# Hybrid decoder block on one core: one product for both sines, gate biases once a block, row scaling by ScalarE, and the mLSTM's maxima spread over the partitions by TensorE

## The chip, the cores and the metric

One core of a Trainium2 chip runs the whole program. The metric is the device time of one execution in microseconds (us). Before the change the median of three runs is 2684.09 us (2683.67 to 2686.39). The engines are called as in the profile: PE (TensorE), DVE (VectorE), ACT (ScalarE), POOL (GpSimd) and SP (SyncE, which here only issues DMAs).

## What is computed

A decoder block over 2048 tokens of width 1024: normalised rows go through one wide projection, its parts through a sliding-window attention and an mLSTM side by side, and their gated sum and a SwiGLU follow. The change lies in the key, query and gate part of the projection. Cut to that, the reference is:

```python
h = modulate(rms_norm(x, g_pre_mix[l]), shift_m, scale_m)
proj = h @ w_in[l]
q_a, k_a, v_a, q_m, k_m, v_m, o_m, i_m, f_m, g_a, g_m = jnp.split(proj, split_points, axis=-1)
q_a = rope(q_a.reshape(B, S, N_Q_HEADS, HEAD_DIM), positions)
k_a = rope(k_a.reshape(B, S, N_KV_HEADS, HEAD_DIM), positions)
y_a = sliding_window_attention(q_a, k_a, v_a, attn_sinks[l])
i_pre = i_m + b_if[l][:MLSTM_HEADS]
f_pre = f_m + b_if[l][MLSTM_HEADS:]
h_m = mlstm_chunkwise(q_m, k_m, v_m, i_pre, f_pre)
...
def rope(t, positions):
    t1, t2 = tf[..., :half], tf[..., half:]
    return jnp.concatenate([t1 * cos - t2 * sin, t2 * cos + t1 * sin], axis=-1)
```

Inside the mLSTM a running maximum `m` of each of the 4 heads scales its exponentials; the kernel computes it as one row of 512 numbers a head and block, and needs the values at the ends of its 128-token chunks on all 128 partitions.

## The kernel before

The tokens are worked in 4 blocks of 512 (NT = 4 tiles of 128 each), and the first part of the kernel in two superblocks of two blocks: blocks 0 and 1 from about 58 to 700 us, blocks 2 and 3 from there. The second part, the SwiGLU, is not touched. All large products are made exact by splitting each operand into a high and a low half (`whi` by ACT at L266 or L263, `wlo` by DVE at L267 or L264) and three matmuls (`mm3`), so PE's instructions are mostly triples at L211 into four accumulators `acc`.

A superblock runs through `h` and the projections in this order: queries of the first block (`evac_q`), its keys, values and gates (`evac_kv`, 264 columns), the mLSTM's values (`vm`, evacuated by ACT at L819), then keys and queries of the second block. For each of these a token tile's accumulator is copied by ACT into a `tx` tile (9 buffers, L772, L798, L819), and for keys and queries `rope` (L738) turns it on DVE with five products: two with the sines of half the width (L749, L750), one with the cosines (L751), a difference and a sum (L752, L753). `evac_kv` also makes the difference of a tile's values to those of the tile before, which it keeps in the constant tile `v_last` (L802, L803), and adds the biases to the 4 + 4 gate columns, in two operations a tile (L804, L805). The halves of queries and keys and the values go to DRAM in `at_d` (L766, L793, L806, L808) and come back as one tile `at` a 128 tokens for the attention (L896).

`hprep` (L475) prepares the normalised rows of a block: sums of squares by ACT (L471), an inverse root by POOL (L457, `rs`), the scaling of four tiles of 128x1024 rows by DVE (L492), then PE's transposes and the affine step by ACT (L502 for the high half, L504) and DVE (L505, the low half). In the odd blocks it also makes sums and differences of parts of `h` (L518 to L521), which `hsums` copies into other tiles with a DMA (L529) and splits again with ACT (L535) and DVE (L536).

`gates` (L824) makes the log gates (L827 to L836), transposes them, runs the scan of the maxima on 4 partitions, and collects in `sm` (4x8) the maxima and sums at the chunks' ends. `sm` goes to DRAM (`sm_d`, L865) and is read back with every partition getting all 32 numbers (`mp`, L867). After a pause of `L_SCAN` PE transposes the rows (68 columns a tile), DVE copies them to `cl` (L875) and forms the exponents `ex` from `cl` and `mp` (L878 to L880), and ACT takes their exponential (L881).

`attention` computes the scores from `at` (copied from PSUM by ACT at L927, masked by DVE at L929), their maxima (L934 to L937), the exponentials on ACT (L942, and `es` at L938), their scaling on POOL (L946), and after PE's transposes of them (L216) the product with the values (L955, L968). Two streams of tiles run side by side.

The order is made in two steps. The Python program lays a main line of matmul triples and between them advances side streams (`gates`, `attention`, `hprep` and so on): each stream yields the time after which it is due again, on a clock `now` (L204) that every matmul and transpose advances by an assumed cost, and `tick` steps what is due. The instructions of ACT, DVE, PE and SP keep the program's order only up to L1557 (`pinned`); from there the build may reorder each engine's instructions by its own estimate of readiness, so an edit in one place can move others. Each engine then works strictly in its order. SP's queue holds nearly all DMAs, the prefetch of raw weights (L297) and of the gates' weights (L441) among them.

## Time and profile before

| | |
|---|---|
| median of 3 runs | 2684.09 us |
| the profiled execution, its time | 2684.71 us |
| its span in the profile | 2682.9 us |
| mean granted clock of PE | 0.993 |
| PE busy | 2628.5 us, 98% |
| DVE busy | 1970.2 us, 73% |
| ACT busy | 1298.3 us, 48% |
| POOL busy | 141.8 us, 5% |

The rows of the profile read: line, engine, operation, the tile written, the tiles read, their shape, the count, then the busy time in us, the mean length of one in ns, and the idle time of the engine just before them with what ended it. Rows of a stretch give the busy time of each engine in it, the granted clock of PE (1.00 is full speed), the busy share of the DMA engines and their GB/s. Neighbouring instructions of one engine overlap a little, so the start of one to the start of the next is shorter than the length shown.

### The profile page before, as it was taken

Reading aid. Unit: us, or ns where it says so; the run is one execution under the profiler, and the core shown is the slowest. Engines: PE = TensorE matmul, PEld = TensorE weight load, DVE = VectorE, ACT = ScalarE, POOL = GpSimd, SP = SyncE. Lnnn points to the kernel's source line nnn. Section 1 sums busy time; section 2 is a strip of 40 time slices with the busy share of each in tenths; the row PEclk is TensorE's granted clock in tenths of the full one; section 3 lists DMA queues with packets and bytes.
Section 4 is the critical chain, followed back from the end, with each engine's and each line's share of the span. In section 5 each row is a group of like instructions: output and inputs, shape, how many; then the busy total and the mean of one; then the engine's idle time right before and its main releaser. Section 6 shows DMA issues by size and latency. Waiting matters only on the chain.

```text
span 2682.9 us, 35853 instructions
## 1 busy us (share of the span) xinstructions
PE 2628.5 (98%) x12414; PEld 2139.1 (80%) x12414; DVE 1970.2 (73%) x3854; ACT 1298.3 (48%) x2527; POOL 141.8 (5%) x181
## 2 busy tenths in 40 slices
PE   8899999999998999999999999999999999999998
PEld 6677788888886778888878888888878888888876
DVE  5788887768686988876777777775776667676466
ACT  5566544545764754444654443335654333333444
POOL 1000001201101000110000000000000000000000
PEclk9899999999999999999999999999999999999999
DMA  7663456887575645578675555446675323234556
GB/s 257 193 229 131 152 180 188 282 315 240 189 253 163 208 133 166 184 246 328 218 249 175 180 170 180 137 150 216 217 244 185 107 101 108 97 110 138 195 199 219
DMA packets 353669, 511.89 MB, mean 191 GB/s; under 512 B 25152, under 2 KB 213692, under 8 KB 348240
## 3 DMA queue, kind: packets, MB, share of 16 engines
q1 hardware_dynamic: 335272, 493.82, 55.3%
q10 hardware_dynamic: 18216, 15.79, 1.9%
q8 instruction: 98, 1.61, 0.2%
q14 instruction: 83, 0.68, 0.1%
HBM read 357.12 MB, written 144.02 MB: 187 GB/s over the span
## 4 chain that ended last, share of the span: by engine, by line
PE 62%; DVE 3%; DMA 2%; ACT 1%; issue 0%; POOL 0%; SPq 0%; DVEq 0%; POOLq 0%; ACTq 0%
PE acc L211 41%; PE mix L211 19%; DVE hl L1589 1%; PE mix L216 1%; DMA raw<-ws_d 1%; ACT hl L1588 1%; DMA raw<-as_d 0%; DMA raw<-in_w_ffn_down_dram 0%; DMA w<-x 0%; DVE w L1899 0%; DVE big L1589 0%; DMA raw<-in_w_ffn_gate_dram 0%; DVE big L1912 0%; DVE w L1932 0%; ACT big L1634 0%
## 5 line engine op out<-in xcount | busy, mean ns | idle before, releaser
L211 PE MATMUL acc<-big,hl 128*128 128x512 f32 x3936 | 933.8, 392 | 2.3 <-ACT hl L1588 0.7
L211 PEld LDWEIGHTS acc<-big,hl 128*128 128x128 f32 x3936 | 732.9, 188 | 165.6 <-issue 10.0
L1588 ACT CAST hl<-raw 128x512 fp32r<-128x512 f32 x732 | 440.0, 621 | 506.1 <-PE acc L211 235.7
L1589 DVE TENSOR_TENSOR hl<-raw,hl 128x512 fp32r<-128x512 f32 x732 | 498.4, 696 | 190.0 <-ACT hl L1588 187.8
L211 PE MATMUL acc<-whi,big 128*128 128x512 f32 (+1 forms) x1216 | 355.8, 374 | 9.5 <-ACT big L502 3.6
L211 PE MATMUL mix<-big,hl 128*128 128x512 f32 x1056 | 263.1, 390 | 1.6 <-ACT hl L1588 0.9
L211 PEld LDWEIGHTS acc<-whi,big 128*128 128x128 f32 x1216 | 221.8, 190 | 51.0 <-ACT big L502 3.9
L211 PE MATMUL acc<-hl,hl 128*128 128x512 f32 x1008 | 237.2, 393 | 5.9 <-DVE hl L1589 3.2
L211 PEld LDWEIGHTS mix<-big,hl 128*128 128x128 f32 x1056 | 197.7, 188 | 44.5 <-DVE hl L1589 1.9
L211 PEld LDWEIGHTS acc<-hl,hl 128*128 128x128 f32 x1008 | 187.0, 188 | 51.7 <-DVE hl L1589 8.4
L211 PE MATMUL acc<-wlo,big 128*128 128x512 f32 (+1 forms) x608 | 226.0, 374 | 2.2 <-DVE wlo L267 2.2
L211 PE MATMUL mix<-hl,hl 128*128 128x512 f32 x792 | 182.9, 391 | 3.1 <-DVE hl L1589 1.3
L211 PEld LDWEIGHTS mix<-hl,hl 128*128 128x128 f32 x792 | 147.7, 188 | 37.7 <-DVE hl L1589 4.7
L211 PE MATMUL acc<-big,whi 128*128 128x512 f32 x512 | 157.9, 393 | 0.0
L267 DVE TENSOR_TENSOR wlo<-raw,whi 128x1024 fp32r<-128x1024 f32 (+1 forms) x95 | 108.3, 1141 | 65.0 <-ACT whi L266 59.0
L266 ACT CAST whi<-raw 128x1024 fp32r<-128x1024 f32 (+1 forms) x95 | 93.7, 986 | 109.9 <-PE acc L211 103.8
L211 PEld LDWEIGHTS acc<-wlo,big 128*128 128x128 f32 x608 | 115.4, 190 | 23.3 <-DVE wlo L267 3.8
L457 POOL TENSOR_TENSOR rs<-ms,halves 128x1 f32<-128x1 f32 (+1 forms) x56 | 44.0, 798 | 1639.5 <-DVE ms L455 1630.6
L211 PE MATMUL mix<-hcT4h,hl 128*128 128x512 f32 x352 | 115.6, 389 | 0.7 <-ACT hl L1588 0.7
L211 PE MATMUL acc<-hcT2h,hl 128*128 128x512 f32 x352 | 115.5, 389 | 0.0
L211 PEld LDWEIGHTS acc<-big,whi 128*128 128x128 f32 x512 | 95.4, 188 | 19.2
L211 PE MATMUL acc<-big,wlo 128*128 128x512 f32 x256 | 97.6, 392 | 0.0
(354 smaller groups left out, 3520.9 us busy)
## 6 DMA issues: line engine op xcount, KB each, us to landing
raw<-in_w_in_dram SPq DMA_DIRECT2D x46, 1024.0 KB
as_d<-w SPq DMA_DIRECT2D x154, 256.0 KB
raw<-as_d SPq DMA_DIRECT2D x70, 512.0 KB
raw<-in_w_ffn_gate_dram SPq DMA_DIRECT2D x22, 1024.0 KB
raw<-in_w_ffn_up_dram SPq DMA_DIRECT2D x22, 1024.0 KB
raw<-ws_d SPq DMA_DIRECT2D x40, 512.0 KB
tx<-in_w_ada_dram SPq DMA_DIRECT2D x64, 256.0 KB
g_d<-tx SPq DMA_DIRECT2D x64, 256.0 KB
```

The source lines that it names most:

```text
L211: T.matmul(o, lhsT=lhsT, rhs=rhs, start=start, stop=stop, skip_group_check=resumed)
L216: T.transpose(o, i, ident[:k, :k])
L266: A.copy(hv, src)
L267: V.tensor_tensor(lv, src, hv.bitcast(F32), op=ALU.subtract)
L457: G.tensor_tensor(r[:, :n], ms[:, :n], nhalf[:, :n], op=ALU.pow)
L1588: A.copy(v(hi), src)
L1589: V.tensor_tensor(v(lo), src, v(hi).bitcast(F32), op=ALU.subtract)
```

## The change

Five edits in one diff. (1) In `rope` the two products with the sines become one over the full width; its input is read with the two halves of each head swapped (a step of -1 in that dimension) and the sines are broadcast over both. (2) In `evac_kv` the gate columns are copied raw by ACT into `gt` (two small copies a tile), and `gates` adds both biases for all four tiles in two operations. (3) The difference of values takes the tile before from its own `tx` buffer; only the block's last tile is copied to `v_last`, by ACT. (4) In `hprep` the scaling of rows goes from DVE to ACT. (5) In `gates` the DRAM tile `sm_d` and its two DMAs go: DVE spreads `sm` along a diagonal (`own`, 4x32, zeros elsewhere), one matmul with a matrix of ones puts the sum over the 4 partitions, which is all 32 numbers, on every partition, and DVE copies it from PSUM to `mp`.

```diff
--- before.py
+++ after.py
@@ -489,7 +489,7 @@
                 xb = xbs[i]
                 r = rms_of_rows(xb, vs[i])
                 for t in range(2):
-                    V.tensor_scalar(xb[:, t, :], xb[:, t, :], r[:, t:t + 1], None, op0=ALU.mult)
+                    A.activation(xb[:, t, :], xb[:, t, :], AF.Copy, scale=r[:, t:t + 1])
                     xs.append(xb[:, t, :])
         yield L_HP1[1] if b == 1 else L_X
 
@@ -742,12 +742,11 @@
             raw = raw[:, :W]
             src = raw.rearrange("p (h u f) -> p h u f", u=2, f=32)
             cb = cos[:, t, :].unsqueeze(1).to_broadcast([P, heads * 2, 32])
-            sb_ = sin[:, t, :].unsqueeze(1).to_broadcast([P, heads, 32])
+            sb_ = sin[:, t, :].unsqueeze(1).unsqueeze(1).to_broadcast([P, heads, 2, 32])
             z = tx([P, 512])
             zz = z[:, :W].rearrange("p (h u f) -> p h u f", u=2, f=32)
             rr = raw.rearrange("p (h f) -> p h f", f=32)
-            V.tensor_tensor(zz[:, :, 0, :], src[:, :, 1, :], sb_, op=ALU.mult)
-            V.tensor_tensor(zz[:, :, 1, :], src[:, :, 0, :], sb_, op=ALU.mult)
+            V.tensor_tensor(zz, src[:, :, ::-1, :], sb_, op=ALU.mult)
             V.tensor_tensor(rr, rr, cb, op=ALU.mult)
             V.tensor_tensor(src[:, :, 0, :], src[:, :, 0, :], zz[:, :, 0, :], op=ALU.subtract)
             V.tensor_tensor(src[:, :, 1, :], src[:, :, 1, :], zz[:, :, 1, :], op=ALU.add)
@@ -793,16 +792,21 @@
                     nc.sync.dma_start(at_d[n_][:, AT_K:AT_V].rearrange("p (i u k) -> p i u k", i=2, u=2)[:, :, u, :], kk.bitcast(F32))
 
         def evac_kv(b):
+            before = [v_last]
+
             def evac(t, ps):
                 raw = tx([P, 392])
                 A.copy(raw[:, :264], ps[:, :264])
                 v, dv = raw[:, 128:256], raw[:, 264:392]
                 n = b * NT + t
                 y = rope(raw, HKV, b, t)
-                V.tensor_tensor(dv, v, v_last, op=ALU.subtract)
-                V.tensor_copy(v_last, v)
-                V.tensor_tensor(gt[:, t, 0:4], raw[:, 256:260], b_if[:, 0:4], op=ALU.add)
-                V.tensor_tensor(gt[:, t, 32:36], raw[:, 260:264], b_if[:, 4:8], op=ALU.add)
+                for i in range(2):
+                    A.copy(gt[:, t, 32 * i:32 * i + 4], raw[:, 256 + 4 * i:260 + 4 * i])
+                V.tensor_tensor(dv, v, before[0], op=ALU.subtract)
+                before[0] = v
+                if t == NT - 1:
+                    A.copy(v_last, v)
+                    before[0] = v_last
                 nc.sync.dma_start(at_d[n][:, AT_V + P:], dv)
                 if n + 1 < S // P:
                     nc.sync.dma_start(at_d[n + 1][:, AT_V:AT_V + P], v)
@@ -822,6 +826,9 @@
 
 
         def gates(b):
+            for i in range(2):
+                g_ = gt[:, :, 32 * i:32 * i + 4]
+                V.tensor_tensor(g_, g_, b_if[:, 4 * i:4 * i + 4].unsqueeze(1).to_broadcast([P, NT, 4]), op=ALU.add)
             fv = gt[:, :, 32:36]
             e_, u_, d_, l_, n_ = [small.tile([P, NT, 4], F32, tag=f"sp{i}", name=nm("sp"), bufs=1) for i in range(5)]
             V.scalar_tensor_tensor(e_, fv, -1.0, fv, op0=ALU.mult, op1=ALU.min)
@@ -860,15 +867,16 @@
             V.tensor_copy(m_last, mend[:, 3:4])
             V.tensor_copy(sm[:, 4:8], rw[32:36, :].rearrange("p (c t) -> p c t", t=P)[:, :, P - 1])
             negm_d = tc.dram_tile([MH, TB], F32, name=nm("negm_d"))
-            sm_d = tc.dram_tile([MH, 8], F32, name=nm("sm_d"))
             nc.sync.dma_start(negm_d, rw[32:36, :])
-            nc.sync.dma_start(sm_d, sm)
+            own = lf[:, :MH * 8].rearrange("p (h k) -> p h k", h=MH)
+            V.tensor_tensor(own, sm.unsqueeze(1).to_broadcast([MH, MH, 8]), ident[:MH, :MH].unsqueeze(2).to_broadcast([MH, MH, 8]), op=ALU.mult)
             mp = small.tile([P, MH, 8], F32, tag="mp", name=nm("mp"), bufs=2)
-            nc.sync.dma_start(mp, sm_d.unsqueeze(0).to_broadcast([P, MH, 8]))
             yield L_SCAN
             pc_ = mix_tile()
             for t in range(NT):
                 transpose(pc_[:, t * 68:(t + 1) * 68], rw[:, t * P:(t + 1) * P])
+            mm(pc_[:, NT * 68:NT * 68 + 32], ones[:MH, :], own.rearrange("p h k -> p (h k)"), True, True)
+            V.tensor_copy(mp.rearrange("p h k -> p (h k)"), pc_[:, NT * 68:NT * 68 + 32])
             cl = small.tile([P, NT, 3, 4], F32, tag="cl", name=nm("cl"), bufs=2)
             pv_ = pc_[:, :NT * 68].rearrange("p (t w) -> p t w", t=NT)
             for i in range(3):
```

The line numbers after the change are shifted: L492 stays, the sine product is L749, the cosines L750, `vm`'s evacuation L823 (was L819), the score copies L935 (L927), `ex` L886 to L889 (L878 to L881), `es` L946 (L938), the attention's exponentials L950 (L942), the `at` load L904 (L896) and the product's copy L963 (L955). The numbers behind the tiles' names count tiles and are not the same before and after.

How ACT's row reads in block 0, about 105 us into the run, around the exponential `ex` of the maxima and the eight exponentials of the attention's first tile (`tm_1058`, `tm_1059`; afterwards `tm_1047`, `tm_1048`); `mix_1215` (afterwards `mix_1206`) holds the transposed rows of `h` for block 1. Before:

```order
L266 CAST whi_1611<-raw_904 128x528
L881 ACT_TABLE_LOAD
L881 ACTIVATE ex_1133<-ex_1133 128x48
L927 COPY tm_1145<-mix_1165 128x256
L502 ACTIVATE big_966<-mix_1215,sh_162,s_159 128x512
L504 ACTIVATE big_745<-mix_1215,sh_162,s_159 128x512
L942 ACTIVATE tm_1058,sums_1056<-tm_1058,nmx_1055 128x128
L938 ACTIVATE es_1057<-es_1057 128x8
L942 ACTIVATE tm_1058,sums_1056<-tm_1058,nmx_1055 128x128 x3
L942 ACTIVATE tm_1059,sums_1056<-tm_1059,nmx_1055 128x128 x4
```

After:

```order
L266 CAST whi_1555<-raw_893 128x528
L823 COPY tx_1552<-acc_926 128x512
L950 ACT_TABLE_LOAD
L950 ACTIVATE tm_1047,sums_1045<-tm_1047,nmx_1044 128x128
L946 ACTIVATE es_1046<-es_1046 128x8
L950 ACTIVATE tm_1047,sums_1045<-tm_1047,nmx_1044 128x128 x3
L950 ACTIVATE tm_1048,sums_1045<-tm_1048,nmx_1044 128x128 x4
L935 COPY tm_1136<-mix_1156 128x256
L889 ACTIVATE ex_1124<-ex_1124 128x48
L502 ACTIVATE big_957<-mix_1206,sh_162,s_159 128x512
L504 ACTIVATE big_742<-mix_1206,sh_162,s_159 128x512
L266 CAST whi_1602<-raw_893 128x528
```

The attention's exponentials, with the load of their table, now stand ahead of `ex`, and `ex` ahead of L502 and L504, which stood ahead of the exponentials before.

SP's row in block 2, at about 761 us, from the load of the first `at` tile to the copies of `hsums` (L529, `big` to `big`). Before:

```order
L896 DMA at_7491<-at_d_198 128x1792
L297 DMA raw_7735<-in_w_in_dram 128x4x512
L793 DMA at_d_199<-tx_7392 128x2x128
L793 DMA at_d_200<-tx_7392 128x2x128
L806 DMA at_d_201<-tx_7433 128x128
L793 DMA at_d_200<-tx_7415 128x2x128
L793 DMA at_d_201<-tx_7415 128x2x128
L529 DMA big_8022<-big_6899 128x2048
L529 DMA big_8024<-big_6494 128x2048
```

After:

```order
L904 DMA at_7462<-at_d_198 128x1792
L529 DMA big_7995<-big_6881 128x2048
L297 DMA raw_7708<-in_w_in_dram 128x4x512
L792 DMA at_d_199<-tx_7368 128x2x128
L792 DMA at_d_200<-tx_7368 128x2x128
L792 DMA at_d_200<-tx_7389 128x2x128
L792 DMA at_d_201<-tx_7389 128x2x128
L529 DMA big_7997<-big_6476 128x2048
```

The first copy of `hsums` has moved from behind the raw weights (L297) and five stores to a place ahead of them; the second stays behind the stores of keys (L793, afterwards L792), and the store of a value difference (L806) has moved ahead of these rows.

ACT's row in block 3's `hprep`, at about 710 us, where L565 sums the squares of the previous superblock's output rows, L571 scales them and L263 splits the weights of the queries. Before:

```order
L565 ACTIVATE big_6619,sx_6950<-tx_6930 128x512
L565 ACTIVATE tm_6829,sx_6950<-tx_6932 128x512
L565 ACTIVATE big_6619,sx_6991<-tx_6965 128x512
L565 ACTIVATE tm_6848,sx_6991<-tx_6967 128x512
L565 ACTIVATE big_6619,sx_7029<-tx_7006 128x512
L565 ACTIVATE tm_6866,sx_7029<-tx_7008 128x512
L571 ACTIVATE big_6619<-tx_6844,rs_6928 128x512
L571 ACTIVATE tm_6814<-tx_6846,rs_6928 128x512
L263 CAST whi_6972<-raw_6773 128x2x4x64 x2
```

After:

```order
L565 ACTIVATE tm_6830,sx_6973<-tx_6949 128x512
L492 ACTIVATE big_6876<-big_6876,rs_6887 128x1024 x2
L565 ACTIVATE big_6601,sx_7011<-tx_6988 128x512
L492 ACTIVATE big_6878<-big_6878,rs_6896 128x1024 x2
L263 CAST whi_6954<-raw_6755 128x2x4x64 x2
L565 ACTIVATE tm_6848,sx_7011<-tx_6990 128x512
L571 ACTIVATE big_6601<-tx_6826,rs_6910 128x512
L571 ACTIVATE tm_6796<-tx_6828,rs_6910 128x512
L571 ACTIVATE big_6601<-tx_6912,rs_6942 128x512
```

The four scalings of rows (L492, in two rows of two) are new on ACT, among the L565 and ahead of the split L263 and the L571.

## The prediction

> **What bounds the kernel now.** I read the page first: the time by engine, the 40 slices, and the chain that ended last.
>
> ```profile
> span 2682.9 us, 35853 instructions
> PE 2628.5 (98%) x12414; PEld 2139.1 (80%) x12414; DVE 1970.2 (73%) x3854; ACT 1298.3 (48%) x2527; POOL 141.8 (5%) x181
> ...
> PE   8899999999998999999999999999999999999998
> ...
> PEclk9899999999999999999999999999999999999999
> ```
>
> PE is busy for 98% of the span, so a change that leaves every matmul in place can win only where PE waits. The slices show where: in the second and third (67 to 201 us) and around the twelfth and thirteenth. I cut these into stretches of 20 us.
>
> ```profile
> core 0: us, PE busy (x) PEld busy (x) DVE busy (x) ACT busy (x) POOL busy (x), PEclk, DMA share, GB/s
> 60.00:80.00 20.00, 18.94 (x126) 17.20 (x125) 18.58 (x65) 12.20 (x22) 4.35 (x3) 1.00 0.66 208
> 100.00:120.00 20.00, 13.68 (x73) 10.54 (x73) 13.35 (x46) 14.20 (x49) 4.11 (x4) 0.70 0.18 60
> 200.00:220.00 20.00, 20.00 (x116) 16.23 (x117) 18.58 (x48) 14.75 (x42) 2.08 (x2) 1.00 0.47 169
> 700.00:720.00 20.00, 20.00 (x96) 16.66 (x95) 15.76 (x41) 16.67 (x41) 7.86 (x11) 1.00 0.68 220
> 720.00:740.00 20.00, 18.51 (x120) 16.71 (x120) 16.73 (x34) 12.40 (x21) 0.00 (x0) 1.00 0.44 145
> 740.00:760.00 20.00, 18.78 (x113) 16.16 (x111) 19.69 (x61) 14.31 (x25) 0.00 (x0) 1.00 0.81 259
> 760.00:780.00 20.00, 16.68 (x91) 13.90 (x92) 14.57 (x38) 8.39 (x18) 0.00 (x0) 0.93 0.99 348
> 820.00:840.00 20.00, 16.12 (x94) 11.39 (x93) 11.81 (x27) 11.52 (x33) 2.08 (x2) 0.83 0.68 197
> ```
>
> PE idles for 6.3 us of 100:120, 1.5 of 720:740, 1.2 of 740:760, 3.3 of 760:780, 3.9 of 820:840; in 200:220 and 700:720 it is full. The granted clock sinks in the same places. Windows cut at its steps show it binary:
>
> ```profile
> 106.70:108.20 1.50, 0.00 (x0) 0.00 (x0) 0.00 (x0) 0.00 (x0) 0.00 (x0) 0.98 0.45 162
> 108.20:121.80 13.60, 9.38 (x33) 6.83 (x34) 9.14 (x31) 10.60 (x42) 4.11 (x4) 0.50 0.01 2
> 777.20:784.00 6.80, 5.44 (x27) 5.31 (x29) 6.67 (x18) 5.30 (x12) 0.00 (x0) 0.50 0.97 330
> ```
>
> After a gap of some 3 us PE runs at half rate for 6.8 or 13.6 us: the 9.38 us of work in the second row would be 4.7 at full rate, the 5.44 in the third 2.7. So a gap costs itself and, if long enough, as much again.
>
> **The change part by part.** *Maxima without DRAM (block 0).* Rows of the timelines of DVE and PE (start, length, instruction, idle time before it), and who in the whole run waited for the DMA of L867:
>
> ```profile
> 108.35 0.18 DVE L878 SCALAR_TENSOR_TENSOR ex<-cl,mp 128x16 f32<-128x16 f32 x1 [2.32 <-DMA mp<-sm_d]
> ```
>
> ```profile
> 106.03 0.66 PE L216 MATMUL mix<-ident,big 128*128 128x128 f32 x4 [0.53 <-DVE mx L935]
> 110.32 0.59 PE L211 MATMUL acc<-whi,big 128*128 128x264 f32 x1 [3.63 <-ACT big L502]
> ...
> 115.80 0.48 PE L216 MATMUL mix<-ident,tm 128*128 128x128 f32 x1 [1.47 <-POOL tm L946]
> ```
>
> ```profile
>   DVE ex L878: 2.3, 1
> ```
>
> They are one chain: the maxima come back from DRAM at 108.35, DVE has idled for 2.3 us, and behind its `ex` stand the mask copies and `nmx`; ACT idles behind the same `ex`, and L502, for which PE waits 3.6 us, stands behind that. ACT's timeline has the durations:
>
> ```profile
> 105.06 1.28 ACT L881 ACT_TABLE_LOAD   x1
> 109.08 0.24 ACT L881 ACTIVATE ex<-ex 128x48 f32<-128x48 f32 x1 [2.74 <-DVE ex L879]
> 109.48 0.78 ACT L502 ACTIVATE big<-mix,sh,s 128x512 fp32r<-128x512 f32 x1
> 110.82 0.41 ACT L942 ACTIVATE tm<-tm,nmx 128x128 f32<-128x128 f32 x1
> ```
>
> In the new order the exponentials stand ahead of `ex`, and `ex` ahead of L502. They can start when the table is in, at 106.3. Four take 4 x 0.41, so PE's transposes of the first half start near 108.2 instead of after 115.8; the gap that began at 106.7 shrinks from 3.6 to 1.5 us. But L502 now follows eight exponentials (3.3 us), `ex` (0.24) and a copy (0.4): it starts near 110.3 and its product is there at 111.1, where it was at 110.3. Eight transposes fill 0.9 us of that, so a second gap of some 2 us opens at 109.1. The two gaps together equal the old one; what is won is the 1.5 us wait for POOL's product, whose work now lies 3 to 4 us earlier, and some 0.5 of small gaps: 2.0. With no single gap over 2 us the half-rate stretch might go as well (4.7), of which I count half, 2.4. The new matmul (4x128 by 4x32) has no row; between nothing and four passes of a 128x264 matmul (0.12 apart each, 0.5 us) I take 0.1, and its operand is made one DVE instruction after the reductions, with eleven matmuls ahead on PE. In the other three blocks DVE never waited for this DMA (the last row counts one wait). Term: **-4.4**, bounds -6.7 (all of the clock) and +1 (L502 0.8 us later and nothing else won).
>
> *SP's order in block 2.* PE's and ACT's waits in 766 to 786 us, and SP's queue:
>
> ```profile
> PE acc L211 <- ACT tx L819: 3.0, 1, 3.0
> ACT tx L819 <- DMA at_d<-tx: 4.2, 1, 4.2
> ACT big L535 <- DMA big<-big: 2.2, 1, 2.2
> ...
> 761.58 0.38 SPq L297 DMA_DIRECT2D raw<-in_w_in_dram  x1
> ...
> 767.47 1.43 SPq L529 DMA_DIRECT2D big<-big  x2
> ```
>
> L535 copies what L529 brings (1 MB each), behind it on ACT stands the evacuation L819 that frees PE's bank. Now the first L529 is issued ahead of L297's 1 MB and of four stores, near 762.5 rather than 767.5. At the 348 GB/s of 760:780 such a tile (128 x 2048 x 4 bytes) takes 3.0 us, so the copy should be in 3 to 5 us sooner and L535 no longer hold L819. But the DMA engines are full (0.99), the bytes are the same, and the stores that L819's buffers wait for (4.2 us) now come after that megabyte. I take 2 us of the 3.0 and 1 of the 2.7 us of clock: **-3.0**, bounds -5.7 and +3.0 (the stores later by the megabyte).
>
> *One product for two sines, bias once a block, v_last by ScalarE.* The groups' rows:
>
> ```profile
> L749 DVE TENSOR_TENSOR tx<-tx,sin 128x256 f32<-128x256 f32 x16 | 6.7, 421 | 3.6 <-ACT tx L89 2.0 <-PE mix L216 1.0 <-issue 0.6
> L751 DVE TENSOR_TENSOR tx<-tx,cos 128x512 f32<-128x512 f32 x16 | 10.8, 686 | 0.0
> L803 DVE COPY v_last<-tx 128x128 f32<-128x128 f32 x3 | 0.7, 228 | 0.0
> L805 DVE TENSOR_TENSOR gt<-tx,b_if 128x4 f32<-128x4 f32 x4 | 0.7, 168 | 0.0
> ```
>
> Two products of 421 ns become one like L751, 686: 156 ns less, and as the two rows make it a fixed 156 ns beside 1.04 a column, the same for a tile of k. It reads with a step of -1 in one dimension, which no row shows; a price from -156 ns to +156 a tile moves 5 us of DVE time at most, which is seen only where DVE bounds. That is 740:760, at 19.69 of 20 us: there (the last two rows) v_last's copies go, 0.7, and eight bias adds of 168 ns become two, 1.0; the merged products of four k tiles give 0.6. That is 2.3 us of DVE by durations, about half by starts, as neighbours overlap. PE's whole idle time there is 1.2 us. ACT takes over small copies (two a tile, 0.2 each) and is at 14.31 of 20. Term: **-1.0**, bounds -1.2 and +1.
>
> *Rows scaled by ScalarE.* The operation has a row on each engine (L89 is the helper that does it for block 0):
>
> ```profile
> L492 DVE TENSOR_SCALAR big<-big,rs 128x1024 f32<-128x1024 f32 x12 | 8.8, 777 | 0.0
> L89 ACT ACTIVATE big<-big,rs 128x1024 f32<-128x1024 f32 x2 | 2.2, 1132 | 0.0
> ```
>
> Four a block: 3.1 us of DVE against 4.5 of ACT. For block 3 they fall at 712 us, between L565s, ahead of splits of weights that PE needs:
>
> ```profile
> 710.69 0.63 ACT L565 ACTIVATE big<-tx 128x512 f32<-128x512 f32 x1 [1.21 <-DVE tx L562]
> 713.12 0.64 ACT L565 ACTIVATE big<-tx 128x512 f32<-128x512 f32 x1 [1.04 <-DVE tx L562]
> 725.47 0.64 ACT L266 CAST whi<-raw 128x528 fp32r<-128x528 f32 x1
> 726.61 1.09 ACT L773 COPY tx<-acc 128x512 f32<-128x512 f32 x2 [0.50 <-PE acc L211]
> ```
>
> ACT's idle time there is 1.2 + 1.0 us, then none until 726.6. So of 4.5 us some 2.2 are absorbed and 2.3 push L266 and L773. 0.5 us of ACT's own wait takes up a part: **+1.5**, bounds 0 and +4.5. "ScalarE: Activation LUTs" of the Trainium skill, Rules for kernel authors, speaks against this move: multiplications belong on VectorE. By its formula (What ACT_TABLE_LOAD costs: 186 ns + 0.833 a column, 93 more for a pointer) one is 1132 ns, which is the row; if that were all paid by PE the term would be +4.5, by the stage's slack it is not. For block 1 (60:80, DVE 18.58, PE idle 1.1) I take **+0.5**, bounds -1 and +2: L492 waits on POOL's root and stands ahead of splits.
>
> *The rest.* 120 to 700 but for some 2 us, and all from 860, is full of matmuls as in 200:220, so later or earlier work on the other engines changes nothing. Attention of block 2 (820:840) keeps its order on PE: 0, bounds -3 and +3.
>
> Sum: -4.4 - 3.0 - 1.0 + 1.5 + 0.5 = -6.4, span 2676.5. The profiled execution took 2684.7, 1.8 beyond its span, and 0.6 over the median of 2684.1: 2678.3, and 2677.7 beside the median. A measurement of this kernel can tell about 0.2%, 5.4 us.
>
> **The rivals.** *The waits only change places* (27%). In block 0 the two gaps equal the old one by my own sum, and if PE then waits for the second stream's exponentials, which stand behind L502 as before, nothing is won there; in block 2 the engines of DMA stay full. For it: 0.99 and the eight exponentials ahead of L502. Against: DVE's 2.3 us idle do go. Terms 0, 0, -1, +1.5, +0.5: 2685.
>
> *ACT becomes the bound* (20%, the slower side). At 712 to 731 us ACT has no idle time but the 2.2 us counted; DVE's earlier end is useless. If L492 also waits for POOL's root (7.86 us busy in 700:720), everything behind is later by more than 3 us, and PE's gap passes the length that brought the half rate. Price: a gap of 4 us and 4.7 of clock where the forecast has 1.5, with nothing won at 775 and no clock at 107: 2684.1 - 2.0 - 1.0 + 0.5 + 4.0 + 4.7 = 2690. It decides from a push of about 3 us.
>
> *The clock stays up* (15%). If no gap is over 2 us at 107 or 775, both half-rate stretches go whole: -6.7 - 5.7 - 1.0 + 1.5 + 0.5 = -11.4, 2672.7. "TensorE: Matmul & The Clock Gate" of the Trainium skill, Part 1, has it so: half rate after at least one idle window of 3413 ns, windows that run free. Stretches of 13.6 and 6.8 us, four and two windows, agree; and by that rule two gaps of 2 us never trip it. Against: the gap at 775 was 3.04 us, shorter than a window, and did.
>
> **How the numbers follow.** The forecast has 38%; it lies 1 us beyond the 0.2%, so 24 of these count as faster and 14 as the same. With the clock's 15 faster has 0.39; with 25 of the first rival's 27, the same has 0.39; its other 2 and ACT's 20 make slower 0.22. The range runs from the clock's case with block 2's attention 3 us better, 2669, to ACT's, 2691.
>
> **What would show it.** Right: no `mp` among DVE's waits; PE's idle in 100:120 at 4 us or less, PEclk there over 0.8; L529's first start near 762.5 and no PE wait near 775 over 1 us. Wrong: PE waiting for L502 or an L266 split for 3 us, a PEclk under 0.9 in 720:740, DVE durations of the sine product over 842 ns, or a time outside the range.

## The result, and the profile after

The changed kernel took 2692.26 us (median of 9 runs, 2688.52 to 2696.55) and the one before 2684.35 (9 runs, 2678.81 to 2686.39): a ratio of 1.003, 95% interval 1.0022 to 1.0038. It is slower, by 8 us or 0.3%. The forecast was 6.4 us faster, and the time lies above its range.

The page after, by engine and slices:

```profile
span 2690.6 us, 35820 instructions
PE 2638.3 (98%) x12422; PEld 2141.8 (80%) x12422; DVE 1955.9 (73%) x3778; ACT 1314.4 (49%) x2575; POOL 137.2 (5%) x181
...
PE   8999999999998999999999999999999999999998
...
PEclk9999999999999999999999999999999999999999
```

DVE has 14.3 us less to do and ACT 16.1 more, as the diff says. The second slice's clock rose from 8 to 9: the half-rate dip of block 0 shrank from 13.65 to 3.41 us. PE is busy 9.8 us longer, though only 8 records of small matmuls were added. A wide matmul lasts 0.39 us in the records and starts 0.23 after its neighbour, so a stall of up to 0.16 us counts as busy: the busy column hides part of the loss, and what follows goes by starts.

The same stretches of 20 us after:

```profile
core 0: us, PE busy (x) PEld busy (x) DVE busy (x) ACT busy (x) POOL busy (x), PEclk, DMA share, GB/s
60.00:80.00 20.00, 17.32 (x117) 15.36 (x117) 13.98 (x40) 15.72 (x31) 5.54 (x3) 1.00 0.58 174
100.00:120.00 20.00, 16.25 (x110) 12.90 (x108) 17.26 (x51) 17.12 (x55) 4.16 (x4) 0.98 0.24 76
...
700.00:720.00 20.00, 19.07 (x89) 15.39 (x88) 12.99 (x35) 17.30 (x39) 5.91 (x9) 1.00 0.59 193
720.00:740.00 20.00, 18.26 (x109) 15.47 (x108) 13.55 (x25) 15.83 (x27) 1.01 (x2) 1.00 0.52 176
740.00:760.00 20.00, 18.07 (x115) 15.76 (x116) 17.93 (x44) 10.84 (x24) 0.00 (x0) 1.00 0.79 240
760.00:780.00 20.00, 17.94 (x84) 13.94 (x82) 10.56 (x31) 9.88 (x21) 0.00 (x0) 0.91 0.79 249
```

PE gained at 100:120 (16.25 us busy at a clock of 0.98, where it was 13.68 at 0.70) and lost in 60:80 and in every row from 700 to 760. ACT is busier in 60:80 (15.72, was 12.20) and DVE idler. The next rows say who PE waits for: us in total, how many times, the longest. First 60:82, before, then after:

```profile
PE acc L211 <- ACT tx L798: 1.1, 1, 1.1
```

```profile
PE acc L211 <- ACT tx L799: 2.2, 2, 1.3
PE acc L211 <- DVE wlo L267: 0.5, 1, 0.5
```

Then 700:762, before, then after:

```profile
PE acc L211 <- DVE wlo L267: 2.2, 2, 1.5
PE mix L216 <- DVE tx L753: 0.8, 1, 0.8
```

```profile
PE acc L211 <- ACT tx L799: 1.9, 1, 1.9
PE acc L211 <- ACT whi L263: 0.9, 1, 0.9
PE mix L216 <- ACT big L492: 0.9, 2, 0.5
...
```

The larger ones are for ACT now. To place the loss I gave each matmul form its usual distance from start to start in before, and asked when PE of another kernel had done the same work. This is by how many us each stretch of before's time got longer (a single profile carries some 1 us of chance in a stretch, more beyond 862 us, so a place counts where several kernels repeat it; the labels are those of the runs below; e12's profiled execution took 2683.02 us, 4.4 over its median, so its row understates what e12 wins):

```
stretch    62-82 82-100 100-130 130-310 310-700 700-735 735-762 762-790 790-862 862-1000
after       +2.3   +0.7    -6.5    +3.4    -0.2    +2.4    +2.2    +1.1    +1.3     +2.8
e12         -0.2   +1.8    -8.1    +2.3    -0.2    -0.4    -0.4    -0.5    +2.1     +0.1
e17         -0.1   +1.1    -8.1    +2.0    -0.3    -0.3    -0.1    -1.3    +0.8     +0.2
e14         -0.2   +1.1    -6.7    +2.4    -0.3    +4.2    -2.6    -3.0    +1.0     +1.4
e13         +2.3   +0.7    -6.5    +2.6    +0.8    +0.2     0.0    -1.6    +1.1     -0.6
e18         +2.2   +0.7    -7.5    +3.6    -0.3    +4.2    -2.6    -4.0    -0.2     +1.7
e15         +1.9   +1.0    -7.2    +2.3    +0.8    +2.4    +2.8    +1.5    +1.2     +0.5
e1          +1.7   +1.0    -5.0    +0.6    -0.2    +2.4    +0.4    -3.2    -2.0     +3.2
e2           0.0    0.0    -2.2    +2.7    -0.2     0.0    -0.1    +4.7    +2.0     +2.5
e4          -0.2   +1.1    -4.5    +1.6    -0.3    -0.4    -0.1    -0.2    -1.1     +6.4
```

### The profile page after: what moved, and what is told of

Its sections match the earlier page's. It is cut to its first block, busy times and chain, and to the rows that moved or that the text cites. A ratio compares the mean times of both kernels' runs of the same rounds, so it can differ in the third digit from the quotient of the medians.

```text
span 2690.6 us, 35820 instructions
## 1 busy us (share of the span) xinstructions
PE 2638.3 (98%) x12422; PEld 2141.8 (80%) x12422; DVE 1955.9 (73%) x3778; ACT 1314.4 (49%) x2575; POOL 137.2 (5%) x181
## 4 chain that ended last, share of the span: by engine, by line
PE 86%; DVE 6%; DMA 3%; ACT 3%; issue 1%; POOL 0%; ACTq 0%; SPq 0%; DVEq 0%; POOLq 0%
PE acc L211 60%; PE mix L211 23%; PE mix L216 2%; DVE hl L1597 1%; DMA at_d<-tx 1%; PE mix L89 1%; PE acc L89 1%; ACT tm L950 1%; ACT hl L1596 1%; DMA raw<-as_d 1%; DMA raw<-ws_d 0%; DVE wlo L267 0%; DVE big L536 0%; DMA at<-at_d 0%; DVE w L1907 0%
## 5 line engine op out<-in xcount | busy, mean ns | idle before, releaser
L266 ACT CAST whi<-raw 128x1024 fp32r<-128x1024 f32 (+1 forms) x95 | 93.6, 986 | 117.9 <-PE acc L211 105.8
```

Of the source, the lines that this page charges most:

```text
L266: A.copy(hv, src)
```

## The experiments

**The theory**, from the trace after: the rows scaled by ScalarE cost far more than the 2.0 us I gave them, by pushing ACT's evacuations and splits. **Its rivals**: another part is to blame; or any edit that makes the scheduler write another order costs some us; or the new order separates attention's neighbouring matmuls. Ratios are to before, with 95% intervals. 0.1% is 2.7 us.

### Each part alone

e1: before with only this.

```diff
-                    V.tensor_scalar(xb[:, t, :], xb[:, t, :], r[:, t:t + 1], None, op0=ALU.mult)
+                    A.activation(xb[:, t, :], xb[:, t, :], AF.Copy, scale=r[:, t:t + 1])
```

> The kernel before with one edit: rows scaled by ScalarE. If ScalarE's queue is the cause (the four scalings stand ahead of the query halves at 65 us and of the weight splits at 712 us, and PE waits): slower than before by 3 to 5 us, 2687 to 2689, with ACT's waits for a tx buffer (at_d<-tx) near 75 us over 2 us. If the cause is the longer life of the value tiles: within 1 us of before. If no edit counts by itself and the new order of the other instructions does: anywhere within 5 us of before, but not in these places.

e2: before with only the maxima by `own`, `mm` and a copy.

```diff
-            nc.sync.dma_start(sm_d, sm)
+            V.tensor_tensor(own, sm.unsqueeze(1).to_broadcast([MH, MH, 8]), ident[:MH, :MH].unsqueeze(2).to_broadcast([MH, MH, 8]), op=ALU.mult)
...
-            nc.sync.dma_start(mp, sm_d.unsqueeze(0).to_broadcast([P, MH, 8]))
...
+            mm(pc_[:, NT * 68:NT * 68 + 32], ones[:MH, :], own.rearrange("p h k -> p (h k)"), True, True)
+            V.tensor_copy(mp.rearrange("p h k -> p (h k)"), pc_[:, NT * 68:NT * 68 + 32])
```

> The kernel before with one edit: maxima spread by PE. By the profile after, the stage of 100 to 130 us is 6 us shorter, of which 3 to 4 are lost again before 250 us. If those are lost because of the other edits: faster than before by 5 to 6 us, about 2679. If the main line has to wait at 250 us for something that no edit of block 0 brings forward: within 2 us of before.

e3: before with only the gates' bias once a block and `v_last` by ScalarE.

```diff
...
-                V.tensor_copy(v_last, v)
-                V.tensor_tensor(gt[:, t, 0:4], raw[:, 256:260], b_if[:, 0:4], op=ALU.add)
-                V.tensor_tensor(gt[:, t, 32:36], raw[:, 260:264], b_if[:, 4:8], op=ALU.add)
+                for i in range(2):
+                    A.copy(gt[:, t, 32 * i:32 * i + 4], raw[:, 256 + 4 * i:260 + 4 * i])
...
+                V.tensor_tensor(g_, g_, b_if[:, 4 * i:4 * i + 4].unsqueeze(1).to_broadcast([P, NT, 4]), op=ALU.add)
```

> The kernel before with two edits: bias once a block, and the values' tile before taken from its own buffer. If the longer life of the value tiles is the cause (nine tx buffers, evacuations of keys and of the mLSTM's values wait for one): slower by 3 to 5 us, 2687 to 2689, with ACT's waits for at_d<-tx at 740 to 800 us longer than the 5.7 us of before. If ScalarE's rows are: within 1 us of before.

e4: before with only the one product for both sines.

```diff
...
-            V.tensor_tensor(zz[:, :, 0, :], src[:, :, 1, :], sb_, op=ALU.mult)
-            V.tensor_tensor(zz[:, :, 1, :], src[:, :, 0, :], sb_, op=ALU.mult)
+            V.tensor_tensor(zz, src[:, :, ::-1, :], sb_, op=ALU.mult)
```

> The kernel before with one edit: one product with the sines. By its durations (488 ns against two of 326 in the mean) DVE wins 5 us of which 1 us lies where DVE is full: 2683 to 2685 by either theory of a cost. Over 3 us from before would speak for the new order of the rest as a cause of its own.

| run | ratio | 95% | median us |
|---|---|---|---|
| e1 rows | 1.0004 | 0.9996 to 1.0013 | 2684.21 |
| e2 maxima | 1.0023 | 1.0012 to 1.0033 | 2691.17 |
| e3 gates and values | 1.0028 | 1.0016 to 1.0039 | 2689.70 |
| e4 sines | 1.0014 | 1.0006 to 1.0023 | 2687.24 |

This seemed to speak against the theory: alone, the rows cost nothing, and the three others, which I had priced at a gain, cost 4 to 8 us each. The four add up to 0.69%, over twice the whole change: parts do not add here. The table of stretches shows why e1 is even: its rows do cost 1.7 us in 62-82 and 2.4 in 700-735, but with its order the half rate of block 0 lasts 3.41 us instead of 13.65 (-5.0 at 100-130), and 3.2 us are won in 762-790. PE's waits of e1 in 66 to 78 us, then in 706 to 745, are those of the change:

```profile
PE acc L211 <- ACT tx L798: 1.6, 2, 1.3
...
```

```profile
PE mix L216 <- ACT big L492: 0.9, 2, 0.5
PE acc L211 <- ACT whi L263: 0.9, 1, 0.9
...
```

### Is it any new order?

e5 and e6: before with one of the two pauses longer by which generators give way; no instruction is added.

```diff
-L_GATE, L_SCAN = 1800.0, 5500.0
+L_GATE, L_SCAN = 1800.0, 6100.0
```

> The kernel before with no edit, but a planner constant moved (L_SCAN 5500 to 6100), which reorders a few instructions on PE, DVE and ACT around the maxima and changes no work. Theory of the order (each edit costs because the order of before, cut into attention's matmul pairs, is better than its neighbours): slower than before by 2 to 6 us. Theory of the edits (each costs by its own instructions): within 1.5 us of before.

```diff
-L_ROPE, L_ROPEK, L_QK, L_ATT2 = 5000.0, 2100.0, 1500.0, 3500.0
+L_ROPE, L_ROPEK, L_QK, L_ATT2 = 5000.0, 2100.0, 1700.0, 3500.0
```

> The kernel before with no edit, but another planner constant moved (L_QK 1500 to 1700): some rows of PE and SP change places. Theory of the order: slower than before by 1 to 6 us. Theory of the edits: within 1.5 us of before.

e7 (before) and e8 (the change): the scheduler may move nothing on TensorE, whose matmuls stand in the order in which the program was written.

```diff
-            if not pinned[0]:
+            if not pinned[0] and self.eng is not nc.tensor:
```

> The kernel before, with PE held to the order in which the program issues, so that attention's two matmuls on the two halves of the array always stand together. By both theories this kernel is the base of the next one; its attention products should take less of PE's time than the 74.5 us of before (by 4 to 10), and what PE waits more for that is open: 2675 to 2710.

> The changed kernel, with PE held to the program's order as in the run before. Theory of the order (the loss came from attention's matmuls cut into more pieces on PE): no slower than that run, or faster by 1 to 6 us, as the chain through DRAM is gone. Theory of the edits: slower than that run by 5 to 9 us, as the change is slower than before.

e5 came out at 1.0003 (0.9994 to 1.0012) and e6 at 0.9996 (0.9987 to 1.0006): these two small shifts of order are worth nothing. They test large ones poorly: up to 1000 us they move 20 to 33 of PE's 4917 records, where e1 moves some 1000. e7 is 1.0725 (1.071 to 1.074), e8 1.0768 (1.0754 to 1.0783). So the scheduler's order of matmuls is worth 7%; and with it taken away the change still costs, 2890.36 against 2878.31 us, 12 us. So a loss of this size needs no new order of matmuls, though this base is another kernel, 7% slower. The rival that any new order costs is answered further down: e12, e14 and e17 have new orders too, and are faster than before.

### Attention's pairs of matmuls

In e9 (the change) and e10 (before) the score and value products of attention are kept in program order behind the first of a group, so that neighbours on the two halves of the array stay neighbours; e11 takes them apart.

```diff
-        T.matmul(o, lhsT=lhsT, rhs=rhs, start=start, stop=stop, skip_group_check=resumed)
+        ins = T.matmul(o, lhsT=lhsT, rhs=rhs, start=start, stop=stop, skip_group_check=resumed)
+        if pin:
+            tc.keep_in_program_order(ins)
...
```

> The changed kernel, with the matmuls of attention's scores held in the program's order behind one another, so that the two halves of the array stay paired: in the order 180 neighbouring pairs where the changed kernel has 129 (before 140), for ten more switches between attention and the projections. Theory of the pairs (the change lost time because it cut attention's pairs): 51 x 0.11 less some 1 us, so 4 to 5 us faster than the changed kernel, 2687 to 2688. Theory that the pairs are hidden or do not count: 2691 to 2694.

> The kernel before, with the same holding of attention's scores: 178 pairs where it had 140, for 28 more switches. Theory of the pairs: 4 us less 3, so 1 us faster than before, 2682 to 2684. Otherwise within 2 us of before or slower by what the holding makes PE wait.

```diff
-                    for lt, rt, st_, sp_ in ((qth, kth, True, False), (qth, ktl, False, False), (qtl, kth, False, True)):
-                        for g in range(2):
-                            pr = slice(g * 64, (g + 1) * 64)
+                    for g in range(2):
+                        pr = slice(g * 64, (g + 1) * 64)
+                        for lt, rt, st_, sp_ in ((qth, kth, True, False), (qth, ktl, False, False), (qtl, kth, False, True)):
```

> The kernel before, with the scores of one half of the heads issued ahead of the other half's: 83 neighbouring pairs where before has 140, everything else as before. Theory of the pairs, each 0.11 us: 6 us slower, 2689 to 2691. If pairs are hidden beside other waits: within 2 us of before.

e9 was 1.0066 (1.0054 to 1.0079), 0.36% slower than the change; e10 1.0022 (1.0013 to 1.0031); e11 1.0007 (0.9998 to 1.0016). Counted as neighbours of one shape that start less than 0.05 us apart in the trace, 165 pairs ran together after and 189 in before. e9 had 207 and e10 210, more than either, and both were slower than the kernels that they came from; holding the order may cost something itself. e12 below has 176, fewer than before, and is faster. So the pairs don't decide the time. e11 was a weak test: its trace has 182 pairs, only 7 fewer than before.

### The change with one part taken back

e12: the change, but with `V.tensor_scalar` for the rows, as before. e15: the change, but with `v_last` copied by VectorE for each tile, as before. e16: before with the rows, gates and values of e1 and e3 together.

```diff
-                    A.activation(xb[:, t, :], xb[:, t, :], AF.Copy, scale=r[:, t:t + 1])
+                    V.tensor_scalar(xb[:, t, :], xb[:, t, :], r[:, t:t + 1], None, op0=ALU.mult)
```

> The changed kernel with the scaling of rows back on VectorE; the order has 143 pairs. Theory that ScalarE's queue costs (gaps near 72 and 716 us): 3 to 4 us faster than the change, 2688 to 2689. Theory of the pairs: 14 more pairs and 8 fewer switches, 2 to 3 us faster, 2689 to 2690. If neither: 2692.

```diff
...
-                if t == NT - 1:
-                    A.copy(v_last, v)
-                    before[0] = v_last
+                V.tensor_copy(v_last, v)
```

> The change, but with v_last copied for every tile by VectorE as before, so that a key tile's buffer is free as early as before. Theory that late rows cost much only because the value tiles hold buffers (evacuations near 757 us wait 3.3 us for one): 5 to 7 us faster than the change, 2685 to 2687. Theory that ScalarE's lateness is enough: within 2 us of the change, 2690 to 2694.

```diff
+                    A.activation(xb[:, t, :], xb[:, t, :], AF.Copy, scale=r[:, t:t + 1])
...
+                    A.copy(v_last, v)
...
```

> The kernel before with three edits: rows on ScalarE, bias once a block, value tiles. If their costs add: 0 + 5.6, 2689 to 2690. If rows and value tiles make each other worse: 2694 to 2700. If the sine and maxima edits are needed for it: 2684 to 2688.

e12 is 0.9983 (0.9974 to 0.9992), 2678.64 us: faster than both kernels. Against the change that is 0.47%, 12.6 us, with some 3 us of uncertainty from the two intervals. The expectation had 2 to 4 us. So in the company of the other parts the rows cost 12.6 us, and the others together, which had looked bad one by one, win 4.6 (2.1 to 7.0). e15 is 1.0018 (1.0009 to 1.0027), e16 1.0000 (0.9991 to 1.0009): taking back the values helps by 0.12%, at the edge of what the intervals can tell, and leaves most of the loss, and e16 shows again that parts don't add (1.0004 and 1.0028 alone).

### Which block's rows?

e13, e14, e17, e18: the change, with the rows on ScalarE in block 1, 3, 2, and in 1 and 3.

```diff
+                    if b in (1,):
+                        A.activation(xb[:, t, :], xb[:, t, :], AF.Copy, scale=r[:, t:t + 1])
+                    else:
+                        V.tensor_scalar(xb[:, t, :], xb[:, t, :], r[:, t:t + 1], None, op0=ALU.mult)
```

> The change, but rows scaled by ScalarE only in block 1 (VectorE in blocks 2 and 3). Theory of the two places (ScalarE's queue near 72 us costs 2 to 3 us, near 712 to 780 us some 9): 2681 to 2682. Theory that any rows on ScalarE shift the whole order and cost as a lottery: no place, 2677 to 2692.

> The change, but rows scaled by ScalarE only in block 3. Theory of the two places: 2687 to 2690, with PE waiting for L492 and the split L263 near 717 to 725 us and for the keys' evacuation near 757 us. Theory of the lottery: 2677 to 2692 without these waits.

> The change, but rows scaled by ScalarE only in block 2, where PE is full while they run. Theory that block 2's rows cost by the order they set for the stage of 740 to 780 us: 3 to 6 us slower than the change without rows, 2682 to 2685, with the loss at 740 to 780 us. Theory of places (no wait there, no cost): 2678 to 2680.

> The change, but rows scaled by ScalarE in blocks 1 and 3 and by VectorE in block 2. If the places' costs add (block 1's 9, block 3's 1.7 by the medians): 2688 to 2690. If block 2's rows are needed for the change's 2692: at most 2688. If blocks 1 and 3 do it together: 2691 to 2693.

| rows on ScalarE in | run | ratio | 95% | median us |
|---|---|---|---|---|
| none | e12 | 0.9983 | 0.9974 to 0.9992 | 2678.64 |
| block 1 | e13 | 1.0011 | 1.0003 to 1.0020 | 2687.48 |
| block 2 | e17 | 0.9983 | 0.9975 to 0.9992 | 2679.44 |
| block 3 | e14 | 0.9982 | 0.9973 to 0.9991 | 2680.38 |
| 1 and 3 | e18 | 1.0003 | 0.9994 to 1.0012 | 2683.65 |
| all | change | 1.0030 | 1.0022 to 1.0038 | 2692.26 |

Block 1's rows cost 0.28% beside none (e13) and 0.21% beside block 3's (e18 against e14), 6 to 8 us. Block 2's or 3's alone cost nothing. All three cost 0.27%, 7 us, more than 1 and 3. My theory for e13 and e14, some 9 us for block 3's rows and 2 to 3 for block 1's, had it the wrong way round. Waits of PE in 66 to 78 us, e12, then e18 (whose lines lie 3 further down):

```profile
PE acc L211 <- DVE wlo L267: 0.8, 1, 0.8
```

```profile
PE acc L211 <- ACT tx L802: 2.1, 2, 1.3
```

How this comes about is seen on ACT of the change, from 64 to 76 us:

```profile
64.91 2.19 ACT L492 ACTIVATE big<-big,rs 128x1024 f32<-128x1024 f32 x2 [0.61 <-POOL rs L457]
67.00 1.55 ACT L762 ACTIVATE tx<-mix 128x512 fp32r<-128x512 f32 x3
68.43 2.19 ACT L492 ACTIVATE big<-big,rs 128x1024 f32<-128x1024 f32 x2
70.51 1.05 ACT L266 CAST whi<-raw 128x1024 fp32r<-128x1024 f32 x1
71.45 0.39 ACT L799 COPY tx<-acc 128x264 f32<-128x264 f32 x1
...
75.39 0.38 ACT L799 COPY tx<-acc 128x264 f32<-128x264 f32 x1 [2.29 <-DMA at_d<-tx]
```

The first pair of L492, with 0.6 us for POOL's root ahead of it, stands ahead of the high halves of the queries (L762), which begin at 67.00, where before begins them at 64.67 (its L763). The second pair stands ahead of a split (L266) and of the first evacuation of keys (L799). So the queries' halves are stored later. SP's queue, before, then after:

```profile
65.29 1.61 SPq L766 DMA_DIRECT2D at_d<-tx  x3
67.27 0.38 SPq L297 DMA_DIRECT2D raw<-in_w_in_dram  x1
```

```profile
67.60 0.34 SPq L765 DMA_DIRECT2D at_d<-tx  x1
68.12 0.37 SPq L297 DMA_DIRECT2D raw<-in_w_in_dram  x1
68.58 3.24 SPq L765 DMA_DIRECT2D at_d<-tx  x5
```

Before, three of these stores stand ahead of a load of raw weights, in the change one. The store issued at 68.58, behind the load, lands 6.7 us later; e12's second and third, ahead of it, take 2.3. The trace gives this store as what the second evacuation of keys waits for, 2.29 us. Before, the second starts at 71.70 without a wait, and only the third waits for a store:

```profile
74.21 0.38 ACT L798 COPY tx<-acc 128x264 f32<-128x264 f32 x1 [2.14 <-DMA at_d<-tx]
```

So shortly before 75 us ACT has emptied one accumulator of keys in the change and two in before, and PE stands:

```profile
71.89 0.50 PE L211 MATMUL acc<-whi,big 128*128 128x512 f32 x1 [0.90 <-ACT tx L799]
72.87 0.50 PE L211 MATMUL acc<-wlo,big 128*128 128x512 f32 x1 [0.48 <-DVE wlo L267]
...
75.82 0.50 PE L211 MATMUL acc<-whi,big 128*128 128x512 f32 x1 [1.30 <-ACT tx L799]
```

One store ahead of the load and a second evacuation that waits are found in each of the seven traced kernels with block 1's rows on ACT (in e15 too, which holds no value tile longer), three stores and a third that waits in all the others that keep the scheduler's order.

2.7 us in these three gaps, where before waits 1.1 and e12 0.8: most of the +2.3 of the table, which is seen with block 1's rows on ACT and with nothing else (1.4 to 2.3 in seven kernels, 0 to -0.2 in the others). Block 3's rows cost 2.4 to 4.2 at 700-735 in each kernel that has them and nothing in the others. In e14 and e18 that is 4.2, as PE there runs at half rate for 3.41 us from 717 or 720 (1.7 us), and given back by 790 (-2.6 and -3.0 or -4.0); in the change it isn't, and 735 to 790 loses 3.3 more. That is where the change and e18 part: +3.3 there against -6.6. Three blocks on ACT don't bring this loss by themselves: e1 has -2.8 there and e16, by the same working, -1.4. Of the kernels with three, those that lose there (the change, e15) have the sine product and the new maxima as well; e2, with the maxima alone, loses 4.7 at 762-790, and e12, with both and no rows on ACT, loses nothing there. Block 2's rows run at 663 to 669 us in e17, and PE waits for none of them there; that with them the scheduler writes another order for what follows is my reading, and not shown.

## Why the prediction was wrong, point by point

**Rows scaled by ScalarE: the step that failed.** I priced "of 4.5 us some 2.2 are absorbed and 2.3 push L266 and L773" at +1.5, and block 1 at +0.5, bounds -1 and +2. Undoing it gives 12.6 us instead of 2.0. Where it lies:
- Block 1. I looked at PE's idle time and DVE's load in 60:80, and gave the term its size from ACT's free time. But L492 was not put into ACT's free time; it was put ahead of the queries' halves and of an evacuation. The halves' stores fell behind a load in SP's queue, and the second evacuation of keys waited for a buffer that such a store frees. The path is ACT's halves, SP's store, the buffer, ACT's evacuation, PE's bank. By place that is 2.3 us, by the ratios 6 to 8. The profiles can't place the difference: the profiled executions of e13 and e12 are 3.1 us apart (2686.11 and 2683.02), their medians 8.8.
- Block 3. At 700-735 the term was mis-sized: +1.5 forecast, 2.4 to 4.2 measured, within its own bounds. There PE waits for the L263 split and for L492 itself, not for L266 and L773.
- The rest appears once all three blocks are on ACT beside the other parts: 0.27% more than blocks 1 and 3, 7 us, placed at 735 to 790. That was in no term: I priced a new instruction as so much added work in a place. That the scheduler's new order of what follows makes this loss is my reading, and no run shows it.

The rule of "ScalarE: Activation LUTs" in the Trainium skill (Rules for kernel authors) that multiplications belong on VectorE agrees with the time of the twelve together. The page's formula gives 1132 ns, and 12 of these paid in full would be 13.6 us, near the 12.6; but the runs don't bear that reading out, since the four of block 2 and the four of block 3 cost nothing alone.

**SP's order in block 2 (-3.0): didn't come.** The order was as I read it, the time wasn't. SP's queue after, then the row of before that corresponds to the first of these:

```profile
767.49 0.33 SPq L904 DMA_DIRECT2D at<-at_d  x1
767.91 0.53 SPq L529 DMA_DIRECT2D big<-big  x1
768.54 0.54 SPq L297 DMA_DIRECT2D raw<-in_w_in_dram  x1
769.17 6.69 SPq L792 DMA_DIRECT2D at_d<-tx  x4
```

```profile
761.14 0.33 SPq L896 DMA_DIRECT2D at<-at_d  x1
```

L529 was to start near 762.5 and started at 767.91. It stands behind the load of `at`, which needs the last key stores; these came late, because the evacuations did. ACT shows both ends of it:

```profile
759.02 0.38 ACT L799 COPY tx<-acc 128x264 f32<-128x264 f32 x1 [3.32 <-DMA at_d<-tx]
...
777.38 1.14 ACT L535 CAST big<-big 128x512 fp32r<-128x512 f32 x2 [7.14 <-DMA big<-big]
778.42 0.58 ACT L823 COPY tx<-acc 128x512 f32<-128x512 f32 x1
```

ACT idles 7.14 us for the copy, and L823, for which PE waits (2.1 us in all), stands behind it: a wait moved, as the first rival had it. Was that only due to the late rows? e12's queue, then its copy and PE's wait in 762:785:

```profile
757.88 0.33 SPq L904 DMA_DIRECT2D at<-at_d  x1
758.30 0.53 SPq L529 DMA_DIRECT2D big<-big  x1
```

```profile
767.95 2.19 ACT L535 CAST big<-big 128x512 fp32r<-128x512 f32 x4 [3.75 <-DMA big<-big]
```

```profile
PE acc L211 <- ACT tx L823: 2.7, 2, 2.0
...
```

There L529 starts 9.6 us sooner than in the change, and PE still waits 2.7 us for L823; 762-790 gains 0.5. So the step was too high by itself too. I had also mis-sized the copy: from the 348 GB/s I took 3.0 us for one, and ACT gets it 9.5 us after its issue in the change, 9.6 in e12 and 8.1 in before. The 3 to 4 us that e1, e14 and e18 win there come with a clock that stays full; but e4 has that too and wins 0.2, so the clock alone isn't it.

**Maxima without DRAM (-4.4): right in place, its size partly luck.** 100-130 got 6.5 us shorter, within the bounds of -6.7 and +1. ACT's chain came out as worked out (exponentials from 106.3, L502 near 110.3):

```profile
106.62 0.40 ACT L950 ACTIVATE tm<-tm,nmx 128x128 f32<-128x128 f32 x1
...
110.07 0.24 ACT L889 ACTIVATE ex<-ex 128x48 f32<-128x48 f32 x1
110.21 0.77 ACT L502 ACTIVATE big<-mix,sh,s 128x512 fp32r<-128x512 f32 x1
```

PE's didn't: its transposes of the exponentials start at 110.15, not 108.2, behind 0.82 us of waiting for POOL's product (L954), and one gap of 2.92 us, longer than the 2 that I allowed, opens at 114.77, for L963. PE idled 3.75 us in 100:120 at a clock of 0.98, and DVE no longer waits for the DMA. But e2, with this edit alone, wins 2.2 there, which is the chain's 2.0; the half rate stays in it (10.2 us from 108.7). And e1 and e4, without the edit, win 5.0 and 4.5, as their orders leave 3.41 us of the dip. So the clock's share is not this edit's own. And 3.4 us are lost again in 130-310, where I had counted nothing; e2 has 2.7 of them.

**DVE's relief at 740:760 (-1.0)** was smaller than that even where the rows don't hide it: DVE's 19.69 us busy fell to 17.93, but e12 and e17 have only -0.4 and -0.1 at 735-762, within the chance of one profile. In the change it is lost to the late evacuation at 759 us. The sine product has the price I took, 686 ns, reversed read and all:

```profile
L749 DVE TENSOR_TENSOR tx<-tx,sin 128x512 f32<-128x512 f32 x16 | 10.9, 688 | 3.6 <-ACT tx L89 2.0 <-PE mix L216 1.5
```

**The rivals.** "ACT becomes the bound" (2690) came nearest to 2692, and its cause is the right one, ACT's queue; but not its place or its clock: at 720:740 PEclk is 1.00, and most of the cost lies in block 1 and behind 735. "The clock stays up" happened in part: half-rate stretches fell from 30.7 us in all to 20.5, worth 5 us, and the kernel still got slower. Of the terms but the rows I had -8.4, and e12 measured -4.6 (-7.0 to -2.1): too good by half, mostly for SP's step (-3.0 forecast, -0.5 in e12's row).

One reading of the page was loose and changes no term: of the slices that I named only the thirteenth shows below 9 for PE and only the second in the clock; the third and the twelfth don't.

**What stays open:** why all three blocks' rows cost 7 us more than those of 1 and 3, which of the scheduler's choices does it, and why e2, e3 and e4 lose alone what they win together. The table places the first at 735 to 790 and no more.

## What to carry to other kernels

An operation moved to an engine with free time is priced by what stands behind it in that engine's queue, not by the engine's share: look for copies whose stores free the buffers that a later evacuation needs, and for what those stores then stand behind. Where a scheduler orders the program, test a change by taking parts out of it as well as by trying them alone; here the parts alone came to +0.69%, all of them to +0.30%, and the same without one part to -0.17%. A version that keeps the rows on VectorE (e12), or moves only those of block 2 or 3 (e17, e14), beats both kernels at 0.9982 to 0.9983.

## What the runs showed of the hardware

A gap of under 2 us can bring the half rate. In the change PE stood still once between 755 and 761 us, for 1.91 us:

```profile
759.46 0.50 PE L211 MATMUL acc<-whi,big 128*128 128x512 f32 x1 [1.91 <-ACT tx L799]
```

```profile
760.90:764.10 3.20, 3.20 (x10) 2.42 (x10) 3.20 (x8) 1.98 (x5) 0.00 (x0) 0.50 0.38 100
```

In e18 a gap of 1.80 us, with two of 0.26 and 0.49 ahead of it, did the same at 720 us:

```profile
719.36 1.48 PE L211 MATMUL acc<-whi,big 128*128 128x512 f32 x4 [1.80 <-ACT whi L263]
```

```profile
720.20:723.40 3.20, 3.20 (x9) 2.51 (x8) 0.44 (x1) 3.20 (x6) 0.00 (x0) 0.50 0.73 280
```

My case for no dip below 2 us was wrong, and so was the point from which that rival was to decide. "TensorE: Matmul & The Clock Gate" of the Trainium skill, Part 1, asks for at least one idle window of 3413 ns. The lengths agree, 3.41, 6.83, 10.24 and 13.65 us in these traces; the threshold does not, and here the measurement decides. The gap of 2.92 us at 114.8 of the change was followed by 3.41 us, those of before by 6.83 and 13.65, so the length of a gap alone doesn't set the length of the dip. Nor does it decide whether there is one: a gap of 1.91 us at 837.99 in the change, as long as the one above, leaves the clock at full rate until 846.1, and e12's gap of 2.33 us at 115.77 brings no dip at all. Sums say more than single gaps: in the 3.41 us ahead of the dip PE idled 1.91 us in the change (760.8), 2.1 in e18 (720.1), 1.7 in before (777.2) and 1.7 in e2 (108.7), there in two gaps of 0.86 and 0.87. These are four places, and not a rule.
